# Splitting the first matmul of each seven-product group into two of 128 columns

## The chip, the cores and the metric

The kernel runs on one core of one Trainium2 chip. The metric is the device time of one execution in microseconds (us); the time of a kernel is the median of its runs.

## What is computed

The reference is a decoder trunk of two layers on 512 tokens of width 1024, in float32. Each layer has three sublayers, and the change lies in the first and the third of them, the half feed-forward networks (FFN):

```python
def swiglu(x, w_in, w_out):
    gate, up = jnp.split(x @ w_in, 2, axis=-1)
    return (jax.nn.silu(gate) * up) @ w_out

for l in range(DEPTH):
    h = layer_norm(ALPHA * h + 0.5 * swiglu(h, ffn1_in[l], ffn1_out[l]), ln_g[l, 0], ln_b[l, 0])
    mix = hybrid_mixer(h, ...)
    h = layer_norm(ALPHA * h + mix, ln_g[l, 1], ln_b[l, 1])
    h = layer_norm(ALPHA * h + 0.5 * swiglu(h, ffn2_in[l], ffn2_out[l]), ln_g[l, 2], ln_b[l, 2])
```

The hidden width of an FFN is 2816, which is 22 tiles of 128 columns for the gate and 22 for the up branch.

## The kernel before, in words

**Three matmuls for one product.** Weights and activations are float32. Each is held as a high part in float32r, rounded by a copy on ScalarE (ACT), and a low part, the difference, made on VectorE (DVE) (`Weights.parts`, L130 to L132). `mm3` (L341 to L345) does one block product as three float32r matmuls: activations' high part by the weights' high part (L343), low by high (L344) and high by low (L345), or with the sides changed where activations are the stationary operand. Every matmul instruction is issued with a load of its stationary operand, 128 columns; the profile lists these loads as an engine of their own, PEld. The first two matmuls of an `mm3` have the same stationary operand, and each loads it.

**Seven products in place of eight.** Most of the first matmul of an FFN, `x @ w_in`, is done in groups of four weight tiles (two gate, two up) by a Strassen-like scheme. In each group the 2 by 2 block product of weights and activations is made from seven block products of sums of blocks. `ffn` (L510) calls `quad` (L675) once for each group: 7 times in the first FFN of a layer and 9 times in the second, so 32 times in all over the two layers. The sums of activation blocks are made once per FFN (`x_sums`, L629), the sums of weight blocks for each group on GpSimd (POOL) and DVE (`quad_item`, L163).

**One product.** The inner function `product(i, bank, item, half, start)` (L682) does one of the seven: for the two halves g (gate and up) and four blocks k of 128 rows it calls `mm3` on 256 columns of the accumulation bank, 24 matmuls of 256 columns. So a group has 168 matmuls. The order of the products in a group is fixed in the code (L699 to L710): 1 into bank `qa`, 5 into `qc`, 6 into `qb`, 2 into `qa`, 4 into `qd`, 7 into `qb`, 3 into `qc`. A start flag stands on the first matmul of a bank only (L691: `first` needs `start`, k = 0 and g = 0); it clears the marks of the whole bank, so that the first matmul on the other 256 columns, which has no flag, overwrites too.

**Order around the change.** The instructions of each engine run in the order in which the program issues them. After product 1 the closing work of the group before is issued (`before()`, ACT and DVE), then product 5 and so on. The split weights stand in a ring of slots in SBUF; a product's last use of an item frees its slot (`W.done`, L206) and so lets the next item be made. Items of the groups are placed 16 elements further in a slot than the plain units (`SHIFT`, L33, L105). In front of the groups of an FFN stand pairs of plain units with 512-column matmuls into `g` and `u` (`pair`, L528), and in front of these, at the change of sublayer, plain units with 256-column matmuls into `hd` (L469 to L476), with transposes into `tx` (L414) between them.

Other matmuls that the text speaks of: L1196 in the attention (float32r, 64 columns each, into `cs`), L1101 in the state-space part (plain float32, 128 columns each, into `sx`; there are 16 such instructions with `er` over the two layers, and the profile has 32 records of them, two for each), L1234 (float32r, 256 columns, right behind L1196).

Of the kernel before, what the change touches and what calls it, by code (L numbers as in the profile page):

```python
# [216 lines left out]
class Trunk:  # L217
# [457 lines left out]
    def quad(self, u, xs, ap, op, acts, before):  # L675


        nc, ve, W = self.nc, self.nc.vector, self.W
        at = {n: u + i for i, n in enumerate(Weights.QUAD)}
        ba, bb, bc, bd = (self.bank(n) for n in ("qa", "qb", "qc", "qd"))  # L680

        def product(i, bank, item, half, start):  # L682
            xh, xl = xs[i]
            for g in range(2):
                n = item if item == "x4" else item + "gu"[g]
                wh, wl = W.get(at[n])
                o = bank[:, 256 * g:256 * g + 256]
                for k in range(4):
                    w = slice(512 * (g if item == "x4" else half) + 128 * k,
                              512 * (g if item == "x4" else half) + 128 * k + 128)  # L690
                    first, last = start and k == 0 and g == 0, k == 3 and g == 1  # L691
                    self.mm3(o, wh[:, w], wl[:, w], xh[:, k], xl[:, k], first, last, not start)
                if (i, item) in ((6, "x2"), (2, "x1"), (3, "x3")) or (item == "x4" and g == 1):
                    W.done(at[n], full=True)

        vw = op.tile([128, 2, SEQ], F32, tag="vw", name="vw")
        u2 = op.tile([128, SEQ], F32, tag="u2", name="u2")
        v, w = vw[:, 0], vw[:, 1]
        product(1, ba, "x1", 0, True)  # L699
        if before:  # L700
            before()
        product(5, bc, "x2", 0, True)
        nc.scalar.activation(v, ba, AF.Copy)
        product(6, bb, "x2", 1, True)
        nc.scalar.activation(w, bc, AF.Copy)
        product(2, ba, "x1", 1, False)
        ve.tensor_tensor(u2, v, bb, op=ALU.add)  # L707
        product(4, bd, "x4", 0, True)
        product(7, bb, "x3", 0, False)
        product(3, bc, "x3", 1, False)  # L710

        def after():
            a = ap.tile([128, 2, SEQ], F32, tag="u", name="aq")
            acts.append(a)
            ve.tensor_tensor(v, v, bb, op=ALU.add)
            ve.tensor_tensor(w, w, v, op=ALU.add)
            ve.tensor_tensor(v, v, bd, op=ALU.subtract)  # L717
            ve.tensor_tensor(u2, u2, bc, op=ALU.add)
            g, p = slice(0, 256), slice(256, 512)
            nc.scalar.activation(a[:, 0, g], ba[:, g], AF.Silu)  # L720
            nc.scalar.activation(a[:, 1].rearrange("p (i n) -> p i n", i=2), vw[:, :, g], AF.Silu)
            nc.scalar.activation(a[:, 0, p], u2[:, g], AF.Silu)
            ve.tensor_tensor(a[:, 0, g], a[:, 0, g], ba[:, p], op=ALU.mult)
            ve.tensor_tensor(a[:, 1].rearrange("p (i n) -> p i n", i=2),
                             a[:, 1].rearrange("p (i n) -> p i n", i=2), vw[:, :, p], op=ALU.mult)
            ve.tensor_tensor(a[:, 0, p], a[:, 0, p], u2[:, p], op=ALU.mult)

        return after
# [947 lines left out]
```

## Time and profile before

| | us |
|---|---|
| median of 3 runs | 1900.32 |
| lowest and highest run | 1898.56 and 1900.52 |
| the profiled execution's own time | 1899.04 |
| span of its profile, first to last instruction | 1897.1 |

The profile is of one execution. Its span leaves out about 2 us at the two ends of the execution. Engines are named PE (TensorE's matmuls), PEld (TensorE's weight loads), DVE, ACT, POOL and SP. A timeline row gives the start and the duration of an instruction in us, its engine, line and operation, what it writes and reads, the shape, and in brackets the idle time of the engine ahead of it and what ended that. Matmuls overlap: the duration of one is longer than the distance to the next. The type is shown as f32 for float32 and float32r alike in matmul rows.

### The profile page before, as it was taken

The numbers are of one execution on the slowest core, as the hardware profiler recorded it, in microseconds if no ns is written. First come the engines' busy times: TensorE is split into PE (matmuls) and PEld (weight loads), VectorE is DVE, ScalarE is ACT, GpSimd is POOL, SyncE is SP. The second block draws the span as 40 slices with busy tenths as digits, with TensorE's granted clock in tenths as the row PEclk, the third lists the DMA queues.
The fourth block names the chain that finished last, engine by engine and source line by source line (L and its number), as shares of the span: only waits on it lengthen the run. The fifth ranks groups of instructions, "written<-read, shape, count | busy, mean of one in ns | idle before, by whom it ended". The sixth has DMA issues, their size and how long they took to land.

```text
span 1897.1 us, 30481 instructions
## 1 busy us (share of the span) xinstructions
PE 1875.3 (99%) x12164; PEld 1672.4 (88%) x12164; DVE 1372.8 (72%) x1926; ACT 810.6 (43%) x1388; POOL 527.4 (28%) x539
## 2 busy tenths in 40 slices
PE   9999999999999999999999999999999999999998
PEld 7999878888788999998899998788977889999886
DVE  8998524767976899864598984346779678999534
ACT  5444323135771444543234543231458614455430
POOL 3332940114321322300042329301223232232001
PEclk9999999999999999999999999999999999999999
DMA  7233434022112123343203333340311211332421
GB/s 254 90 111 113 129 111 144 32 94 68 56 37 98 62 96 111 112 169 125 85 23 112 112 125 93 128 138 21 115 46 45 84 51 67 112 112 90 167 89 45
DMA packets 57214, 183.59 MB, mean 97 GB/s; under 512 B 11248, under 2 KB 12016, under 8 KB 57072
## 3 DMA queue, kind: packets, MB, share of 16 engines
q1 hardware_dynamic: 57072, 181.64, 28.6%
q8 instruction: 96, 1.57, 0.3%
q14 instruction: 46, 0.38, 0.1%
HBM read 179.19 MB, written 2.10 MB: 96 GB/s over the span
## 4 chain that ended last, share of the span: by engine, by line
PE 81%; POOL 8%; DVE 7%; DMA 2%; issue 1%; ACT 1%; SPq 0%; DVEq 0%; ACTq 0%; POOLq 0%
PE o L491 26%; PE qb L345 3%; PE qb L343 3%; PE qb L344 3%; PE qa L345 3%; PE qa L343 3%; PE qa L344 3%; PE qc L345 3%; PE qc L343 3%; PE qc L344 3%; PE o L1314 2%; PE pt L1298 2%; PE qd L345 2%; PE qd L343 2%; PE qd L344 2%; DVE ring L132 1%
## 5 line engine op out<-in xcount | busy, mean ns | idle before, releaser
L132 DVE TENSOR_TENSOR ring<-st,ring 128x1024 fp32r<-128x1024 f32 (+1 forms) x257 | 358.3, 1402 | 255.3 <-ACT ring L131 252.9
L131 ACT ACTIVATE ring<-st 128x1024 fp32r<-128x1024 f32 (+1 forms) x257 | 269.9, 1054 | 364.4 <-PE o L491 148.2
L491 PE MATMUL o<-ring,ap 128*128 128x512 f32 x1440 | 331.4, 391 | 3.5 <-ACT ap L602 3.3
L491 PEld LDWEIGHTS o<-ring,ap 128*128 128x128 f32 x1440 | 271.0, 188 | 61.5 <-ACT ap L602 4.1
L383 POOL TENSOR_TENSOR mv<-mv,expo 128x1 f32<-128x1 f32 x24 | 35.6, 1481 | 577.3 <-DVE mv L382 577.3
L182 POOL TENSOR_TENSOR st<-st,sb 128x512 f32<-128x512 f32 x64 | 96.6, 1510 | 187.0 <-DVE ring L132 119.3
L343 PE MATMUL qb<-th,ring 128*128 128x256 f32 x512 | 144.4, 282 | 0.3 <-DVE u L707 0.3
L344 PE MATMUL qb<-tl,ring 128*128 128x256 f32 x512 | 144.3, 282 | 0.0
L345 PE MATMUL qb<-th,ring 128*128 128x256 f32 x512 | 144.2, 282 | 0.0
L343 PE MATMUL qa<-xh,ring 128*128 128x256 f32 x512 | 143.5, 280 | 0.0
L345 PE MATMUL qa<-xh,ring 128*128 128x256 f32 x512 | 143.5, 280 | 0.0
L344 PE MATMUL qa<-xl,ring 128*128 128x256 f32 x512 | 143.5, 280 | 0.0
L491 PE MATMUL o<-wh,ap 128*128 128x512 f32 x448 | 125.5, 391 | 0.0
L177 POOL TENSOR_TENSOR sumg<-sb 128x512 f32<-128x512 f32 x32 | 51.0, 1595 | 178.0 <-DMA sb<-in_ffn_in 178.0
L491 PEld LDWEIGHTS o<-wh,ap 128*128 128x128 f32 x448 | 83.5, 188 | 17.6 <-DVE vw L717 0.6
L344 PEld LDWEIGHTS qb<-tl,ring 128*128 128x128 f32 x512 | 98.8, 193 | 0.0
L344 PEld LDWEIGHTS qa<-xl,ring 128*128 128x128 f32 x512 | 98.0, 191 | 0.1
L343 PEld LDWEIGHTS qb<-th,ring 128*128 128x128 f32 x512 | 96.8, 189 | 0.5 <-issue 0.5
L345 PEld LDWEIGHTS qb<-th,ring 128*128 128x128 f32 x512 | 96.9, 189 | 0.0
L132 DVE TENSOR_TENSOR wl<-st,wh 128x1024 fp32r<-128x1024 f32 x51 | 62.8, 1239 | 47.1 <-ACT wh L131 46.9
L343 PEld LDWEIGHTS qa<-xh,ring 128*128 128x128 f32 x512 | 96.1, 188 | 0.2
L345 PEld LDWEIGHTS qa<-xh,ring 128*128 128x128 f32 x512 | 96.1, 188 | 0.0
(459 smaller groups left out, 5163.4 us busy)
## 6 DMA issues: line engine op xcount, KB each, us to landing
st<-in_ffn_in SPq DMA_DIRECT2D x110, 512.0 KB, 3.3
st<-in_ffn_out SPq DMA_DIRECT2D x88, 512.0 KB, 3.3
sb<-in_ffn_in SPq DMA_DIRECT2D x64, 512.0 KB, 3.2
st<-in_w_out SPq DMA_DIRECT2D x16, 512.0 KB, 3.8
st<-in_w_b SPq DMA_DIRECT2D x8, 512.0 KB, 4.4
st<-in_w_a SPq DMA_DIRECT2D x8, 512.0 KB, 5.0
ln_g<-in_ln_g SPq DMA_DIRECT2D x6, 512.0 KB, 4.0
ln_b<-in_ln_b SPq DMA_DIRECT2D x6, 512.0 KB, 5.9
```

The lines of the kernel that those rows point to most:

```text
L131: self.nc.scalar.activation(hi, t, AF.Copy)
L132: self.nc.vector.tensor_tensor(lo, t, hi.bitcast(F32), op=ALU.subtract)
L177: po.tensor_tensor(s[:, f], b[:, f], b[:, r], op=ALU.add)
L182: po.tensor_tensor(a[:, f], a[:, f], b[:, f], op=ALU.subtract)
L343: mm(out, lhsT=ah, rhs=bh, start=start, stop=False, skip_group_check=skip)
L344: mm(out, lhsT=ah, rhs=bl, start=False, stop=False, skip_group_check=skip)
L345: mm(out, lhsT=al, rhs=bh, start=False, stop=stop, skip_group_check=skip)
L383: nc.gpsimd.tensor_tensor(mv[:, 2:3], mv[:, 2:3], self.expo, op=ALU.pow)
L491: mm(ps[t][f], lhsT=a[:, q], rhs=w[:, 512 * f:512 * f + 512], start=(k == first and a is ah and w is wh), stop=end)
L1298: nc.tensor.transpose(ps[:, 128 * k:128 * k + 128], p[:, i, 128 * k:128 * k + 128], ident)
L1314: mm(o[64 * i:64 * i + 64], lhsT=self.v[:, b, k, 64 * g:64 * g + 64], rhs=pt[:, i, 128 * k:128 * k + 128], start=False, stop=b == 1 and k ...
```

## The change

In product 1 of each group (i = 1, which writes `qa` and always has `start`), the first `mm3` (g = 0, k = 0) is written out. Its first matmul, 256 columns, becomes two of 128 columns with the same stationary operand, the first with the start flag and the second without; the other two matmuls of that `mm3` are as before.

```diff
                     first, last = start and k == 0 and g == 0, k == 3 and g == 1
-                    self.mm3(o, wh[:, w], wl[:, w], xh[:, k], xl[:, k], first, last, not start)
+                    if i == 1 and g == 0 and k == 0:
+                        for c in (slice(0, 128), slice(128, 256)):
+                            nc.tensor.matmul(o[:, c], lhsT=wh[:, w], rhs=xh[:, k, c], start=c.start == 0, stop=False)
+                        nc.tensor.matmul(o, lhsT=wh[:, w], rhs=xl[:, k], start=False, stop=False)
+                        nc.tensor.matmul(o, lhsT=wl[:, w], rhs=xh[:, k], start=False, stop=False)
+                    else:
+                        self.mm3(o, wh[:, w], wl[:, w], xh[:, k], xl[:, k], first, last, not start)
```

## Rows read from the trace of the kernel before

**Rows 1.** The page's first part: busy us, share of the span, instructions.

```profile
PE 1875.3 (99%) x12164; PEld 1672.4 (88%) x12164; DVE 1372.8 (72%) x1926; ACT 810.6 (43%) x1388; POOL 527.4 (28%) x539
```

**Rows 2.** Timeline at the start of two neighbouring groups in the first FFN.

```profile
94.61 0.28 PE L343 MATMUL qa<-xh,ring 128*128 128x256 f32 x1
94.61 0.19 PEld L344 LDWEIGHTS qa<-xl,ring 128*128 128x128 f32 x1
94.72 0.28 PE L344 MATMUL qa<-xl,ring 128*128 128x256 f32 x1
...
113.65 0.28 PE L343 MATMUL qa<-xh,ring 128*128 128x256 f32 x1
```

**Rows 3.** Timeline: starts of the first group and of two in the second FFN.

```profile
51.32 0.28 PE L343 MATMUL qa<-xh,ring 128*128 128x256 f32 x1
...
689.27 0.28 PE L343 MATMUL qa<-xh,ring 128*128 128x256 f32 x1
...
709.06 0.28 PE L343 MATMUL qa<-xh,ring 128*128 128x256 f32 x1
```

**Rows 4.** Windows: length, busy PE, PEld, DVE, ACT, POOL (instructions touched); clock, DMA share, GB/s.

```profile
94.60:113.60 19.00, 19.00 (x170) 19.00 (x169) 17.13 (x21) 9.79 (x13) 6.99 (x4) 1.00 0.33 112
171.50:191.30 19.80, 19.80 (x170) 19.80 (x169) 15.09 (x22) 7.40 (x11) 0.00 (x0) 1.00 0.43 131
649.70:827.80 178.10, 178.10 (x1514) 178.10 (x1513) 156.16 (x176) 89.95 (x118) 47.35 (x32) 1.00 0.35 117
996.00:1134.50 138.50, 138.50 (x1177) 138.50 (x1176) 122.45 (x134) 68.62 (x89) 36.41 (x24) 1.00 0.34 113
1590.40:1768.50 178.10, 178.10 (x1513) 178.07 (x1512) 156.28 (x176) 88.70 (x117) 44.09 (x32) 1.00 0.33 110
1075.10:1094.90 19.80, 19.80 (x170) 19.80 (x170) 18.99 (x21) 10.05 (x13) 5.87 (x4) 1.00 0.34 107
78.50:82.90 4.40, 4.40 (x27) 4.40 (x26) 3.93 (x6) 2.90 (x5) 1.29 (x1) 0.61 0.18 57
```

**Rows 5.** PE's timeline around two waits inside the first two groups.

```profile
65.93 0.36 PE L343 MATMUL qb<-th,ring 128*128 128x256 f32 x1 [0.32 <-DVE u L707]
...
67.04 0.28 PE L343 MATMUL qb<-th,ring 128*128 128x256 f32 x1
67.16 0.28 PE L344 MATMUL qb<-tl,ring 128*128 128x256 f32 x1
...
78.14 0.39 PE L345 MATMUL qc<-th,ring 128*128 128x256 f32 x1 [2.20 <-DVE ring L132]
```

**Rows 6.** PE's timeline in the sixth group of the first FFN.

```profile
155.92 0.28 PE L344 MATMUL qc<-tl,ring 128*128 128x256 f32 x1
156.11 0.39 PE L345 MATMUL qc<-th,ring 128*128 128x256 f32 x1
```

**Rows 7.** Timeline of the 64-column matmuls (eight merged) and what follows them.

```profile
461.14 1.08 PE L1196 MATMUL cs<-kc,qs 128*128 128x64 f32 x8
...
462.02 0.30 PEld L1234 LDWEIGHTS s<-kk,qs 128*128 128x128 f32 x2
462.05 0.37 PE L1234 MATMUL s<-kk,qs 128*128 128x256 f32 x1
```

**Rows 8.** PE's timeline of plain float32 matmuls with 128 columns, two records each.

```profile
401.13 0.39 PE L1101 MATMUL sx<-s5u,er 128*128 128x128 f32 x2
401.36 0.39 PE L1101 MATMUL sx<-s5u,ei 128*128 128x128 f32 x2
```

**Rows 9.** PE's timeline of the 256-column matmuls into `hd` behind transposes.

```profile
609.70 0.36 PE L343 MATMUL hd<-xh,ring 128*128 128x256 f32 x1
...
611.21 0.28 PE L343 MATMUL hd<-xh,ring 128*128 128x256 f32 x1
611.33 0.28 PE L344 MATMUL hd<-xl,ring 128*128 128x256 f32 x1
```

## The prediction

> **What bounds the kernel now.** I read the page's first part first: TensorE (PE) is busy 1875.3 of 1897.1 us, VectorE (DVE) 72% [rows 1]. So a nanosecond added to the matmul stream moves the end, unless it falls ahead of a wait for something else, and one saved counts as long as the weights keep coming. The change touches only the stream of the 32 seven-product groups, 168 matmuls each (7 products of 2 halves, 4 blocks, 3 terms), so I looked next at its pace.
>
> The timeline gives it from start to start (the duration in a row, 0.28 us, contains pipeline depth and is not the pace). One group starts at 94.61 and the next at 113.65: 19.04 us, or 113.3 ns a matmul [rows 2]. Another starts at 689.27 and the next at 709.06: 19.79 us, or 117.8 ns [rows 3]. The work is the same, PE has no gap in either, and the granted clock is 1.00, the 2.4 GHz level, in both [rows 4]. So **the same stream runs at one of two paces**, 0.75 us a group apart. The windows over all groups of three FFNs are slow throughout: 178.1 us for 9 groups, 138.5 for 7 and 178.1 for 9 [rows 4]. With the last group of the first FFN, 19.8 us from 171.5, 26 of 32 are wholly slow.
>
> What sets the pace? Once taken up, it holds over group after group. The groups of each FFN follow a gap-free stream of 512-column matmuls (at 51.32 in the first, [rows 3]) and start slow. The pace changes only where the rhythm breaks. At 65.93 a matmul waits for DVE, with 0.32 us of idle time; a microsecond later the step from 67.04 to 67.16 belongs to a fast stream [rows 5]. At 78.14 another has waited 2.20 us for a weight, then the clock falls towards the 1.2 GHz level (0.61 on average from 78.5 to 82.9, [rows 4]); after both the pace is fast, as at 94.61. At 156.11 a matmul comes 0.19 us after the one before it, and from there on the stream is slow, as in the window from 171.5 [rows 4, 6]. So of four breaks inside groups (the clock's return is one) three ended fast.
>
> **The change, part by part.** The first instruction of each group (256 columns) becomes two of 128, each with its own load of the same weights: 32 more matmuls, 32 more loads, no DMA, nothing on other engines. The old waits move to the first half. The fourth instruction's wait for the low part of the weights comes some 0.1 us later, which helps. No wait is added, so nothing queues behind one.
>
> *Price of a half.* No 128-column matmul of this operand type (float32r) is in the trace. The nearest are the eight 64-column ones of L1196, 461.14 to 462.05: 0.114 us each, the start included; the steady step is 0.112 [rows 7]. That is as long as a fast step of 256 columns, so something other than columns limits it. What, the interval from a load's start to its own matmul's start tells: 0.03 us for L1234 (462.02 to 462.05), which has 64 columns in front, 0.11 us in the fast stream (94.61 to 94.72) with 256 in front [rows 2, 7]. It grows with the columns in front, so it is the streaming time of the matmul ahead. 64 columns stream in 0.03 us, and the step of 0.112 is the weight load's. A half must then cost 0.112 as well, by its load.
>
> Bounds: below, half of a fast step, 0.057 us, if its load hid completely; above, the plain float32 matmul of 128 columns, two records from 401.13 to 401.36, 0.23 us [rows 8]. I take 0.112, since L1196 has the same operand type.
>
> The Trainium skill (TensorE: Matmul & The Clock Gate, LDWEIGHTS) puts a load of 128 columns at 128/1.2 = 107 ns; L1196's step agrees. The same page (Back-to-back issue gap) gives 262 cycles for 256 columns and 134 for 128: by it alone the split costs 6 cycles a group, 2.5 ns, nothing in the sum. L1196's step speaks against that here.
>
> *Direct cost.* In a slow stream 2 x 0.112 - 0.118 = 0.106 us a group, in a fast one 0.111. The first two groups lie ahead of the wait that ends at 78.14, which is for DVE and hides them. That leaves 30 x 0.106 = **+3.2 us**. With the bounds' ends: 30 x (0.114 - 0.118) = -0.1, and 30 x (0.46 - 0.118) = +10.3 us.
>
> *What the break does to the pace.* This is the large term, and the trace shows no break of just this form. The halves are limited by loads, so the instruction after them starts out of step with its load, as after the waits. The effect lies between 0 and 0.75 us a group, and below zero by a third pace (second rival). I take the fast pace, because three of four breaks inside the groups ended there, and this one comes at every group. Some instructions pass until it has settled, say 0.02 us. A slow group then gains 0.75 - 0.11 - 0.02 = 0.62 us.
>
> *Sum.* 26 slow groups x 0.62 = 16.1. The group in which 156.11 lies has about 129 matmuls left there at 4.4 ns, 0.57, less 0.13: 0.4. The three fast groups ahead of it, from 94.61 on, lose 3 x 0.13 = 0.4. That is -16.1 us. DVE, which makes the low parts of the weights, is busy 156.16/9 = 17.4 us a group in the second FFN, but 19.0 in the group from 1075.1 [rows 4]. A period of 19.15 us holds the first and leaves nothing for the second, so I expect small waits for weights in the third FFN and take off 1 us. **-15 us**: from the profiled execution's 1899.0 to 1884. The median shown is 1.3 us above that execution, so on its scale 1885; without waits for weights and settling, 1881 on the lower side.
>
> **The rivals.** *The pace stays*, because the halves are too small a break. For it: neither a change of product nor of operand ever changes the pace. Against it: the 0.19 us step at 156.11, shorter than two halves, did. Then only the direct cost counts, +3.2, 1903.5. If the break also turns the three fast groups and part of a fourth slow, 3.2 x 0.75 = 2.4 more: 1906.
>
> *The break leads to a still slower pace: slower than before.* The matmuls of hd start after 128-column transposes, come off a break at 609.70, and settle at 0.120 us (611.21 to 611.33, [rows 9]). Of the trace's breaks this is the one most like ours. Against it: no group shows 0.120, and hd's weights are unshifted units of the ring, the groups' are shifted by 16 elements. Here it would be 30 x 168 x 2.2 ns = 11.1, plus 3.2, plus 2.4 for lost fast groups: +17, 1917. It decides from a mean pace of 117.1 ns on (0.106 us spread over 168 below 117.8): above it the change is slower, below it faster.
>
> *Only some groups change pace*, as other slots and operands meet the break: with half of them, 13 x 0.62 gained, 13 x 0.106 and 0.4 lost, about -6: 1894.
>
> *A half costs the plain float32 price*, pace unchanged: +10.3, 1911. The 0.03 us for 64 columns speaks against it.
>
> That the change does something else than it says gets nothing: the second half lands in columns that the first half's start flag has cleared, as the second 256 columns of each bank do now.
>
> **How the numbers follow.** Fast pace nearly everywhere 0.50; some groups 0.12; pace stays 0.20; slower pace 0.14; plain price 0.04. A measurement of this kernel tells about 0.2%, 3.8 us, from no change. The first two cases are faster: 0.62. Of "pace stays", 0.14 lies just within the bound and 0.06, with the fast groups lost, beyond it; with the last two, slower has 0.24. Low is 1881; the high end reaches over most of "pace stays", 1905. Left out are the 0.18 of the last two cases. The likeliest case alone has 1881 to 1888.
>
> **What would show it.** qa's first line should show 64 records of 128 columns, the halves 0.11 us apart, and groups should start 19.15 us apart in all FFNs. I am wrong if they start 19.9 apart (pace stays) or 20.3 (slower pace), if waits for DVE ahead of qc eat what the pace gives, or, on the price, if two halves take 0.45 us.

## The result and the profile after

The changed kernel takes **1885.99 us** (median of four runs, 1883.3 to 1888.0); the kernel before beside it takes 1899.44 (four runs, 1897.97 to 1900.52). The ratio is 0.9929, 95% interval 0.9916 to 0.9942. Eleven more runs of the old kernel and six of the changed one in a later series gave 1898.42 and 1882.26, ratio 0.9922 (0.991 to 0.9934). The profile below is of the run of 1888.0 us, the slowest of the changed kernel, with a span of 1886.2; against the span before of 1897.1 it is 10.95 shorter from the first to the last matmul.

The page's first part of the kernel after:

```profile
PE 1863.3 (99%) x12196; PEld 1660.2 (88%) x12196; DVE 1372.3 (73%) x1926; ACT 809.4 (43%) x1388; POOL 528.5 (28%) x539
```

There are 32 more matmuls and 32 more loads than in [rows 1], and PE is busy 12.0 us less. DVE, ACT and POOL did the same work. PE bounds the kernel as before; it got through more instructions in less time.

The timeline of PE at the start of a group in the second FFN of the kernel after, with the start of the next group, answers to [rows 2, 3]. L694 is the split matmul, its two halves merged into one row:

```profile
670.75 0.33 PE L694 MATMUL qa<-xh,ring 128*128 128x128 f32 x2
670.92 0.33 PE L695 MATMUL qa<-xl,ring 128*128 128x256 f32 x1
671.09 0.28 PE L696 MATMUL qa<-xh,ring 128*128 128x256 f32 x1
671.21 0.28 PE L343 MATMUL qa<-xh,ring 128*128 128x256 f32 x1
671.33 0.28 PE L344 MATMUL qa<-xl,ring 128*128 128x256 f32 x1
671.44 0.28 PE L345 MATMUL qa<-xh,ring 128*128 128x256 f32 x1
...
689.92 0.33 PE L694 MATMUL qa<-xh,ring 128*128 128x128 f32 x2
```

From start to start it is 19.17 us where [rows 3] had 19.79. Behind the split the steps are 0.17, 0.12, 0.12, 0.11; from there to the next group all are 113.3 ns on average (162 steps in 18.36 us from 671.56 to 689.92). In this trace 30 of the 32 groups run so from end to end, apart from short waits. The first two turn slow (117.8) at a wait, that of 0.87 us at 66.41 and that of 1.9 us for a weight with the half clock behind it; each time the split of the next group, at 72.14 and at 95.63, ends it.

Windows over the groups of the second, third and fourth FFN of the kernel after answer to [rows 4] (the columns are the same); the last three are of stretches in which the clock fell:

```profile
651.60:824.10 172.50, 172.50 (x1521) 172.42 (x1520) 155.11 (x175) 87.81 (x117) 46.92 (x32) 1.00 0.35 117
993.10:1127.60 134.50, 134.50 (x1184) 134.28 (x1183) 121.60 (x134) 68.74 (x89) 37.76 (x24) 1.00 0.34 114
1585.00:1757.40 172.40, 172.40 (x1522) 172.40 (x1521) 156.75 (x175) 87.37 (x116) 46.58 (x32) 1.00 0.34 113
269.40:276.20 6.80, 5.60 (x13) 4.45 (x14) 4.75 (x6) 5.09 (x7) 0.00 (x0) 0.54 0.66 228
78.30:81.70 3.40, 3.02 (x14) 3.02 (x15) 3.40 (x5) 2.00 (x4) 1.28 (x1) 0.56 0.23 89
1163.70:1167.10 3.40, 3.40 (x20) 3.40 (x20) 0.42 (x1) 1.79 (x3) 3.32 (x6) 0.57 0.66 183
```

The nine groups that took 178.1 us take 172.5; the seven that took 138.5 take 134.5. The clock is 1.00 in both. Aligning the two traces matmul by matmul, the change gains 5.4 us in the second FFN, 3.9 in the third and 5.6 in the fourth: 14.9. The profiled run kept 10.95 of it, because about 4 us went elsewhere: 0.2 in and ahead of the first FFN, 0.6 at a wait (0.46 of idle time) in the `o` matmuls at the end of the second FFN, and 3.1 at places whose code the change does not touch, 269.4 and 1163.7. There the kernel before has, in its own profile:

```profile
270.60:274.00 3.40, 3.36 (x9) 2.39 (x8) 2.80 (x4) 3.08 (x5) 0.00 (x0) 0.50 0.55 182
274.00:277.40 3.40, 3.40 (x16) 2.79 (x16) 2.88 (x4) 1.54 (x3) 0.00 (x0) 0.99 0.82 283
1165.00:1168.40 3.40, 3.40 (x23) 3.01 (x21) 1.82 (x3) 1.06 (x1) 3.40 (x5) 1.00 0.82 282
```

At half the clock (the 1.2 GHz level) a step of 256 columns took 0.213 us in place of 0.113 to 0.118 (in the group at 72.14), so each such stretch of 3.4 us costs up to 1.7 us, where PE is busy in it. The run after has one more of them at 269.4 and one more at 1163.7. The one at 1163.7 is there in the later trace of the changed kernel too, at 1158.2, and not in the one trace of the kernel before; whether it belongs to the change is not shown. The waits of PE after, at the top of their view:

```profile
PE o L491 <- ACT ap L602: 3.8, 2, 2.9
PE qc L345 <- DVE ring L132: 1.9, 1, 1.9
```

The first, 2.9 us long at 270.60, stood at 2.17 before. Neither wait is where the split is.

### The profile page after: what moved, and what is told of

The parts are those of the page before. It is cut to its first block, busy times and chain, and to the rows that moved or that the text cites. A ratio compares the mean times of both kernels' runs of the same rounds, so it can differ in the third digit from the quotient of the medians.

```text
span 1886.2 us, 30545 instructions
## 1 busy us (share of the span) xinstructions
PE 1863.3 (99%) x12196; PEld 1660.2 (88%) x12196; DVE 1372.3 (73%) x1926; ACT 809.4 (43%) x1388; POOL 528.5 (28%) x539
## 4 chain that ended last, share of the span: by engine, by line
PE 79%; DVE 8%; POOL 8%; DMA 3%; issue 2%; ACT 1%; SPq 0%; DVEq 0%; ACTq 0%; POOLq 0%
PE o L491 26%; PE qb L344 3%; PE qb L343 3%; PE qb L345 3%; PE qc L345 3%; PE qc L344 3%; PE qc L343 3%; PE qa L344 3%; PE qa L343 3%; PE qa L345 3%; PE o L1320 2%; DVE ring L132 2%; PE pt L1304 2%; PE qd L343 1%; PE qd L344 1%
## 5 line engine op out<-in xcount | busy, mean ns | idle before, releaser
L343 PE MATMUL qb<-th,ring 128*128 128x256 f32 x512 | 141.8, 277 | 0.9 <-DVE u L713 0.9
L345 PE MATMUL qb<-th,ring 128*128 128x256 f32 x512 | 141.6, 277 | 0.0
L343 PE MATMUL qa<-xh,ring 128*128 128x256 f32 x480 | 132.7, 276 | 0.0
L344 PE MATMUL qa<-xl,ring 128*128 128x256 f32 x480 | 132.6, 276 | 0.0
L345 PE MATMUL qa<-xh,ring 128*128 128x256 f32 x480 | 132.6, 276 | 0.0
L343 PEld LDWEIGHTS qa<-xh,ring 128*128 128x128 f32 x480 | 90.1, 188 | 0.0
L344 PEld LDWEIGHTS qa<-xl,ring 128*128 128x128 f32 x480 | 90.1, 188 | 0.0
L345 PEld LDWEIGHTS qa<-xh,ring 128*128 128x128 f32 x480 | 90.1, 188 | 0.0
```

Source lines behind the costliest of these rows:

```text
L343: mm(out, lhsT=ah, rhs=bh, start=start, stop=False, skip_group_check=skip)
L344: mm(out, lhsT=ah, rhs=bl, start=False, stop=False, skip_group_check=skip)
L345: mm(out, lhsT=al, rhs=bh, start=False, stop=stop, skip_group_check=skip)
```

## The experiments

All splits below are of the changed kernel's form (two halves, the other two matmuls of the `mm3` as they were). Starts and steps are read from PE's timeline of each run. Where no number of runs stands with a time, it is that of one run. The cuts from the code show the lines that matter; `...` stands for the lines that only carry a flag or a number there.

### Does the pace hold by itself? One split in an FFN

```diff
-                late = self.quad(self.unit_at["quad", kind, l, j], xs, ap, op, acts, late)
+                late = self.quad(self.unit_at["quad", kind, l, j], xs, ap, op, acts, late, j == q0)
...
-                    if i == 1 and g == 0 and k == 0:
+                    if i == 1 and g == 0 and k == 0 and kick:
```

> The split only in the first group of each FFN (4 splits in place of 32). Theory: the pace is a state that holds until the rhythm breaks, so one split serves all groups behind it; these start 19.04 us apart with no 0.13 us for a split, and the time is some 28 x 0.13 = 3.6 us under the changed kernel's, about 1882 us; where a wait for weights breaks the rhythm a group may fall back to 19.79 us. Rival: a split acts on its own group alone; then only 4 groups are fast, the others start 19.79 us apart, and the time is about 1897 us.

1886.34 us, median of four (1885.35 to 1890.26), against 1898.33 before on that chip: ratio 0.9936 (0.992 to 0.9953). The timeline of PE, with two group starts of the second FFN and a wait in the fourth:

```profile
666.95 0.28 PE L343 MATMUL qa<-xh,ring 128*128 128x256 f32 x1
...
685.99 0.28 PE L343 MATMUL qa<-xh,ring 128*128 128x256 f32 x1
...
1605.83 0.38 PE L345 MATMUL qc<-th,ring 128*128 128x256 f32 x1 [0.23 <-DVE ring L132]
...
1621.24 0.28 PE L343 MATMUL qa<-xh,ring 128*128 128x256 f32 x1
...
1641.03 0.28 PE L343 MATMUL qa<-xh,ring 128*128 128x256 f32 x1
```

By the time, four splits are not told apart from 32 (ratio 0.9929 and 0.9922). The unsplit groups behind the first are 19.04 apart, exactly the fast group of [rows 2]: the pace, once taken up, stays. So it is a state of the stream, not a property of the split instructions. My 1882 was too low for two reasons. At 19.04 the stream overruns DVE now and then, as the prediction had feared for the third FFN: the group at 705.03 took 19.58, with a wait for DVE in it (0.26 us of idle time). And such a wait is a break too, which can end either way: those in the groups at 92.45, 1103.70 and 1601.13 ended slow (the last is shown: 19.79 from 1621.24 to 1641.03), and nothing set the pace right again until the next FFN. Eleven groups ran wholly slow by it. Splitting every group is a repair at each one; splitting one is cheaper but leaves the relapses.

### Is it the additional instruction? The first matmul twice, whole

```diff
-                        for c in (slice(0, 128), slice(128, 256)):
-                            nc.tensor.matmul(o[:, c], lhsT=wh[:, w], rhs=xh[:, k, c], start=c.start == 0, stop=False)
+                        for n in range(2):
+                            nc.tensor.matmul(o, lhsT=wh[:, w], rhs=xh[:, k], start=n == 0, stop=False)
```

> In each group the first matmul is done twice with all 256 columns (its block product is added twice, so the output is not the reference's): one more instruction and one more load as in the changed kernel, but none that is limited by its load. Theory (the short step limited by its load is what moves the pace): the groups stay slow, 19.90 us apart, about 1903 us. Rival (any additional instruction does it, for instance because a group then has an odd number): 19.17 us apart, about 1886 us.

1900.59 us. PE's timeline at two group starts:

```profile
667.46 0.40 PE L694 MATMUL qa<-xh,ring 128*128 128x256 f32 x2
...
687.37 0.28 PE L694 MATMUL qa<-xh,ring 128*128 128x256 f32 x1
```

19.90 a group: 169 steps of 117.8, the slow pace throughout the last three FFNs. In the first FFN, where waits had made the groups fast, they stayed fast (19.15). One more instruction of the same length changes neither pace: of the 26 that met a slow stream or opened an FFN, none ended fast. What counts is the short one.

### Does the place in the group matter? The form of the split?

```diff
...
-                    if i == 1 and g == 0 and k == 0:
+                    if (i == 6 or i == 1 and kick) and g == 0 and k == 0:
```

> The split moved from product 1 to product 6 (10 us later in the group, behind the place where the groups wait for weights), and in the first group of each FFN also in product 1: 36 splits. Theory: the pace is a state, so the place of the split in the group doesn't matter: groups 19.17 us apart as in the changed kernel, 1886 us; a group that a wait for weights (before the 38th matmul) turns slow is fast again from the 49th on and loses under 0.1 us where the changed kernel loses up to 0.6. Rival (the split works by the change of group, or by product 1's operands): groups at 19.9 us, over 1897 us.

1886.08 us; 19.17 a group with the split at product 6, in all of the last three FFNs, but for waits and for the first group of each, which has two splits (19.30). Those first groups are fast by the split in product 1, so most splits in product 6 have nothing to repair. Four do: the groups at 112.56, 150.98, 782.28 and 1028.02 turn slow at a small wait and fast at the split some ten matmuls behind it. PE's timeline of the third:

```profile
786.86 0.28 PE L344 MATMUL qc<-tl,ring 128*128 128x256 f32 x1
...
787.80 0.33 PE L694 MATMUL qb<-th,ring 128*128 128x128 f32 x2
...
788.37 0.28 PE L344 MATMUL qb<-tl,ring 128*128 128x256 f32 x1
...
797.89 0.28 PE L344 MATMUL qb<-tl,ring 128*128 128x256 f32 x1
```

Eight steps in 0.94 us ahead of the split are 117.5 ns each, 84 steps in 9.52 behind it 113.3. The place in the group does not matter.

```diff
-                        for c in (slice(0, 128), slice(128, 256)):
+                        for c in (slice(0, 64), slice(64, 256)):
```

> The changed kernel with the first matmul split into 64 and 192 columns in place of 128 and 128. Theory: both pieces are shorter than a weight load, each costs a load, and the stream behind them starts out of step with its loads as before: 19.17 us a group, 1886 us, two pieces 0.22 us. Rival (only equal halves hit the fast pace): groups at 19.9 us, about 1901 us.

1883.2 us (one run). PE's timeline:

```profile
1006.32 0.36 PE L694 MATMUL qa<-xh,ring 128*128 128x64 f32 x2
1006.52 0.31 PE L695 MATMUL qa<-xl,ring 128*128 128x256 f32 x1
1006.66 0.28 PE L696 MATMUL qa<-xh,ring 128*128 128x256 f32 x1
```

The 64 columns take 0.03 us until the second piece starts, which then takes 0.17, and L695 0.14: together 0.34, as with 128 and 128 (0.06, 0.11, 0.17). Groups are 19.17 apart again. So the cost of a split is not that of its columns: both cuts cost 0.13 over the 19.04 of an unsplit group, about one more load of 0.11. But the split does not always bring the fast pace: the group at 1025.48 turned slow at a wait of under 0.1 us, the next, at 1045.31, took up its split (steps of 0.029, 0.175, 0.136) and went on at 117.8, 19.89 in all; the one after it was fast.

### The third pace: hd split as well

```diff
-            self.m_tile(u0 + i, hp[i], 0, 256)
+            self.m_tiles([u0 + i], [hp[i]], 0, 256, i != 1)
...
+                if kick and k == 0:
+                    mm = self.nc.tensor.matmul
+                    for c in (c0, c0 + 128):
+                        mm(p[:, c:c + 128], lhsT=wh[:, w], rhs=self.xh[:, k, c:c + 128], start=c == c0, stop=False)
+                    mm(p[:, c0:c1], lhsT=wh[:, w], rhs=self.xl[:, k, c0:c1], start=False, stop=False)
+                    mm(p[:, c0:c1], lhsT=wl[:, w], rhs=self.xh[:, k, c0:c1], start=False, stop=False)
+                    continue
```

> The changed kernel, with the same split also in the 256-column matmuls into hd, in the first matmul of three of the eight tiles of each of the three places (at the start and behind each block of transposes): 9 more splits. Theory: hd's step goes from 0.120 to 0.113 us; 576 matmuls x 0.0067 = 3.8 us less 9 x 0.11 for the splits: about 2.9 us faster than the changed kernel. Rival (the third pace belongs to the place of the weights in the ring, not to the history): 0.120 us again a few steps behind each split, and 1 us slower.

1886.39 us. PE's timeline, ten matmuls behind the split at 611.30:

```profile
612.56 0.28 PE L343 MATMUL hd<-xh,wh 128*128 128x256 f32 x1
612.68 0.28 PE L344 MATMUL hd<-xl,wh 128*128 128x256 f32 x1
```

0.120, as in [rows 9]. My theory fell: `hd` settles at 0.120 whatever it comes off, and no split moves it. The rival, that the weights' place makes the third pace, was left.

### The place alone: groups without the offset, with and without the split

The kernel before, and then the changed kernel, with the groups' items placed like the plain units:

```diff
-        o = 0 if kind == "unit" else SHIFT
+        o = 0
```

> The kernel before, without a split, with the groups' items not shifted by 16 elements in their slots. If the place of the weights decides on the third pace: groups 168 x 0.120 = 20.16 us apart, 32 x 0.37 = 12 us slower than before, about 1911 us. If only the history decides, the groups start as before, 19.79 us apart, about 1899 us.

1924.67 us. PE's timeline without the split:

```profile
719.61 0.28 PE L343 MATMUL qa<-xh,ring 128*128 128x256 f32 x1
719.73 0.28 PE L344 MATMUL qa<-xl,ring 128*128 128x256 f32 x1
...
739.77 0.28 PE L343 MATMUL qa<-xh,ring 128*128 128x256 f32 x1
```

> The changed kernel (32 splits) with the groups' items not shifted in their slots. Theory after the unshifted kernel without a split ran all groups at 0.120 us: the place of the weights sets which paces there are, and the split only chooses between the two that the shifted place has. Then the groups stay at 0.120 us a matmul, at least 20.25 us apart, and the time is 1915 us or more. Rival (a split leads to the fast pace wherever the weights stand): 0.113 us, 19.17 us apart but for waits, under 1900 us.

1921.85 us. PE's timeline with it:

```profile
696.39 0.34 PE L694 MATMUL qa<-xh,ring 128*128 128x128 f32 x2
696.56 0.33 PE L695 MATMUL qa<-xl,ring 128*128 128x256 f32 x1
...
716.65 0.22 PE L694 MATMUL qa<-xh,ring 128*128 128x128 f32 x1
```

The step is 0.120 in every group, with the split and without, after waits of about 3 us too: where nothing is waited for, a group takes 168 x 0.120 = 20.16 without the split and 20.26 with it. At this place there is one pace and nothing to win by a break. Against slow groups the place costs 32 x 0.37 = 12 us; most of the rest of the 26 us are waits inside the groups, 14 us by their starts (8.0 of idle time at `qb` for DVE's `u` alone).

The kernel before with another offset:

```diff
-SHIFT = 16
+SHIFT = 8
```

> The kernel before with the items of the groups placed 8 elements further instead of 16; no split. If any offset against the plain units is enough, the groups step at the same two paces as before: 19.79 us apart in the later FFNs, 1899 in all. Rival: an offset of 8 elements counts as none, as in the run without an offset: steps of 0.120 us, 20.16 us apart or more, about 1924. A third outcome, 19.04 apart from the start of each FFN, would mean that the slow pace belongs to the offset of 16 and not to the rhythm: about 1882. I hold the first two equally likely and the third at one in ten.

1903.79 us. PE's timeline at two group starts:

```profile
710.79 0.28 PE L343 MATMUL qa<-xh,ring 128*128 128x256 f32 x1
...
730.67 0.28 PE L343 MATMUL qa<-xh,ring 128*128 128x256 f32 x1
```

None of the three outcomes: 19.88 a group, 118.3 ns a step, in all 32 groups, also behind the wait of 1.76 us at 78.06 after which the groups of the kernel before step at 113.3. At 0 elements one pace is seen (120.0), at 8 one (118.3), at 16 two (117.8 and 113.3). A split was tried at 0 and at 16, not at 8, so a faster pace at 8 is not excluded. The ring is 8 elements shorter here as well, which moves what lies behind it; `hd`, `g` and `u` kept their steps.

### Can hd have it as well? Three tries

First the four units of `hd` alone are moved by 16 elements, on top of the split in `hd`:

```diff
-        o = 0 if kind == "unit" else SHIFT
+        o = 0 if kind == "unit" and i not in self.shifted else SHIFT
...
```

> The kernel with 9 splits in hd, with hd's four units also shifted by 16 elements in their slots as the groups' items are. If the place sets the third pace: hd's step falls from 0.120 to 0.113 us (0.118 where no split reaches it), up to 3.8 us less than with the splits alone, 1883 us. Rival: hd keeps 0.120 us, because of its activations or its transposes, and the time stays at 1886 us; weights that stand outside the ring can keep it in part.

1886.98 us. PE's timeline:

```profile
612.56 0.28 PE L344 MATMUL hd<-xh,ring 128*128 128x256 f32 x1
612.67 0.28 PE L345 MATMUL hd<-xl,ring 128*128 128x256 f32 x1
...
631.68 0.50 PE L344 MATMUL u<-xh,ring 128*128 128x512 f32 x1 [0.57 <-ACT ring L131]
...
635.44 0.80 PE L346 MATMUL u<-xh,ring 128*128 128x512 f32 x1 [3.03 <-DVE ring L132]
```

`hd` now steps at 113.3, and its three sections of a place take 22.31 us in place of 23.50 in the run with the split alone, so 3 x 1.19 = 3.6 are won (2.6 against the changed kernel, which has no splits in `hd` and takes 23.17). They are lost again in front of the second FFN's groups: there `u` comes 6 us later than in the run with the split alone. Of that 3.6 are waits for weights, most of the rest is a stretch at half the clock behind them:

```profile
633.60:640.40 6.80, 4.96 (x12) 3.94 (x13) 6.80 (x8) 3.75 (x5) 0.00 (x0) 0.53 0.52 183
```

The planner's order of the weights changed with the place: a moved unit may not use the extra slot (`wh` and `wl`, which `hd` had at 612.56 above), and reaches 16 elements into the slot behind its own.

So next every unit in the ring was moved, with the splits in `hd` kept and the extra slot allowed for plain units as before:

```diff
-        o = 0 if kind == "unit" else SHIFT
-        for s in sorted(range(self.slots - (o > 0)), key=lambda s: self.freed[s]):
+        o = SHIFT
+        for s in sorted(range(self.slots - (kind != "unit")), key=lambda s: self.freed[s]):
```

> The kernel with hd's splits, and now every weight in the ring is placed 16 elements further, plain units too, which keep the slot that the other run with hd's units moved had forbidden them. Theory: hd's sections take 22.3 us in place of 23.5 at each of three places (unless a unit lies in the extra slot), no 3 us wait for weights comes in front of u, because that came from the slot; 1886.4 less up to 3.6: 1883, and against the kernel with the change alone 0.998 to 1.000. Rival: the faster hd itself makes the weights late: the wait in front of u (3.0 us, with half clock behind it) comes again, 1887.

1892.67 us, median of five (1889.78 to 1892.82), ratio to before 0.9966 (0.9954 to 0.9978), and 10.4 over the changed kernel on the same chip. The wait in front of `u` is gone, as the theory had it, and `hd` gained 0.5 us a place (1.2 if it stepped at 113.3 throughout: one unit of each place lay in the extra slot and stepped at 0.120, and the units behind it went on at 117.8). But the plain units lost more. One of the lines of `u` in the view by line, first from the run with `hd` split and nothing moved:

```profile
L344 PE MATMUL u<-xl,ring 128*128 128x512 f32 x144 | 56.0, 389 | 0.0
```

and from this one:

```profile
L344 PE MATMUL u<-xl,ring 128*128 128x512 f32 x144 | 57.0, 396 | 0.0
```

7 ns more for each matmul of 512 columns. From start to start, worked out over each trace, `u` steps at 233 ns in place of 227 (405 steps), `g` at 232.7 for 228.2 (403) and `o` at 229.7 for 228.1 (2472): 2.7 + 1.8 + 4.0 = 8.5 us. What 16 elements give the 256-column stream they take from the 512-column ones. Two groups also stayed slow through their split (19.89 at 645.58 and 1582.95), 1.4 us.

Last, plain units at their old place and `hd`'s at the new one in every slot, with the two tiles of the extra slot 16 elements wider for it:

```diff
...
-            return tuple(self.split.tile([128, 1024], F32R, tag=g, name=f"{g}{i}") for g in self.extra)
+            o = SHIFT if i in self.shifted else 0
+            return tuple(self.split.tile([128, 1024 + SHIFT], F32R, tag=g, name=f"{g}{i}")[:, o:o + 1024] for g in self.extra)
```

> Plain units at their old place, hd's four units at the place of the groups (16 elements further) in every slot, the extra slot too, whose two tiles are 16 elements wider for that. Theory: hd steps at 113.3 ns in all its sections (22.3 us a place against 23.5), the 512-column streams at 227 ns again (the run with all units moved had up to 235), no 3 us wait for weights in front of u in the third FFN, since that came from the slot that was forbidden to hd: 3.6 us under the changed kernel, a ratio to before of 0.990 to 0.991. Rival: the weights in front of u come late again because hd is faster, 0.993 as the changed kernel. What I can't exclude: the wider first tile moves the second one by 16 elements, and units with their low parts there may step otherwise.

1915.67 us, median of six (1913.77 to 1921.58), ratio 1.0093 (1.0076 to 1.0111): slower than the kernel before. The view by line:

```profile
L500 PE MATMUL o<-ring,ap 128*128 128x512 f32 x1440 | 338.5, 395 | 0.8 <-ACT ap L611 0.5
```

Here `o` steps at 233.2 ns, 5 over the changed kernel's 228.0 on 2476 steps, 13 us, and `g` and `u` lose 5 ns a step as well (some 400 steps each); 13 of the 32 groups are slow in spite of their splits, two of them from a wait on; and there are waits for weights of 4.5 us at `g` in front of the second FFN and 3.0 at `u` in front of the fourth. So the forbidden slot, which `hd` may use here, was not all that made the weights late. This run shares with the first of the three that `hd`'s units reach 16 elements into the slot behind; that alone was not tried. A tile 64 bytes wider in each partition moved what lies behind it, and the streams that were at their best before no longer are. Which tile's place did it was not tried.

### The changed kernel again

> The changed kernel as it is, for a comparison beside the run before it on one chip: a median of 1886, from 1883 to 1888, as in its first runs, and a ratio to before of 0.993. Where a run lies between those ends goes by the number of windows at about half clock in it: two of them 1884 or lower, four 1888.

1882.26 us, median of six (1880.08 to 1886.8). What I expected of the half clock fell short. The profiled run, the fastest, has three such stretches of about 3.4 us besides its end; the run of 1888.0 has them at three places with one twice as long, about 13.7 us in all, so 1.7 us of the 7.9 between the two. The larger part lies at one place, where the windows of this run show

```profile
269.40:276.20 6.80, 6.80 (x32) 5.63 (x31) 5.81 (x7) 4.55 (x6) 0.00 (x0) 1.00 0.75 254
```

no idle time and the clock at 1.00, where the first run had the wait of 2.9 us for ACT and 6.8 us at half the clock: 6.1 us between them, worked out from the starts around it (0.2 us apart at 230, 6.3 at 332). So one wait that comes or does not, with the clock behind it, makes most of the difference between these two runs. Four of the groups' late steps ended slow over the two traces, six fast; the smallest that ended slow was a single step of 0.13 us, in this run's group at 112.35.

## Why the prediction was right

**The level.** 1885 was forecast and 1886 measured, with faster by 0.7%. The gain of 15 us stood against 13.5 in the first series and 16.2 in the second.

**The price of a half** was right in the sum, not in its parts. The steps were not 0.112 and 0.112: the second half follows 0.06 after the first (it was to be 0.11), L695 0.11 later, L696 0.17 after that. The three steps make 0.34, as forecast (0.112 + 0.112 + 0.113). The timeline of the loads (PEld) of the kernel after, around the start at 670.75, says why:

```profile
670.53 0.19 PEld L345 LDWEIGHTS qc<-xh,ring 128*128 128x128 f32 x1
670.64 0.30 PEld L694 LDWEIGHTS qa<-xh,ring 128*128 128x128 f32 x2
670.86 0.19 PEld L695 LDWEIGHTS qa<-xl,ring 128*128 128x128 f32 x1
670.97 0.19 PEld L696 LDWEIGHTS qa<-xh,ring 128*128 128x128 f32 x1
```

They go on 0.11 apart straight through the split. The first half's short step is the 0.057 of the lower bound, but the loads behind it cannot follow, so the debt is paid two instructions later. The 64 and 192 columns of the other cut gave the same sum. In the fast stream the split thus costs 19.17 - 19.04 = 0.13 us, the 0.11 and 0.02 of the forecast. The cycles of the Trainium skill (TensorE: Matmul & The Clock Gate, Back-to-back issue gap), by which two halves would cost, as an estimate, 2.5 ns more than the whole, are given there for an isolated matmul, and the section itself says that they under-count small ones in a stream with loads. That is so here: the split cost 130 ns. The 107 ns of the Trainium skill (same page, LDWEIGHTS) for a load of 128 columns is near the 0.11 measured.

**The break and the pace**, the large term, came out at the forecast size: 19.79 to 19.17 is 0.62 a group, the number of the sum. The period of 19.15 was 0.02 short. The reason given, a rhythm between loads and matmuls that a short instruction upsets, is supported by three runs: one split per FFN suffices, a whole additional instruction does nothing, the place in the group is indifferent. That this break ends fast rested on three of four breaks in the trace before, which were waits and a change of the clock. Four breaks are few to go by, and waits turned out to be another matter: in the two traces of the changed kernel they ended fast in six of ten cases. So the odds taken were in part luck. The split did better: all 11 that met a slow stream or opened an FFN in these two traces ended fast. It is still not certain: a run each with 64 columns, with everything moved and with the wider tiles has groups that kept 117.8 through their split. One reading was incomplete, too: behind the 0.19 us step at 156.11, which the prediction called shorter than two halves, there is a second late one (the row after [rows 6] starts 0.22 later):

```profile
156.33 0.28 PE L343 MATMUL qc<-th,ring 128*128 128x256 f32 x1
```

What the rhythm is, the loads tell in part. Their view by line, in ns, first in a slow group before (700 to 718), then in a fast one after (672 to 689):

```profile
L344 PEld LDWEIGHTS qb<-tl,ring 128*128 128x128 f32 x16 | 3.1, 192 | 0.0
L343 PEld LDWEIGHTS qb<-th,ring 128*128 128x128 f32 x16 | 3.0, 188 | 0.0
```

```profile
L344 PEld LDWEIGHTS qb<-tl,ring 128*128 128x128 f32 x16 | 3.0, 188 | 0.0
```

In both a load starts 2 to 5 ns behind the matmul ahead of it, so a lasting shift between loads and matmuls is not what tells the paces apart. But in the slow groups every third load takes 192 ns, in the fast ones none, and without the offset, at 120.0, all do. In the run with the first matmul doubled, where a group has 169 instructions, the long load moves on by one term from group to group: the count of three goes on through the stream. The slow groups of the run with wider tiles have no such load, so it is a mark of the slow pace, not shown to be its cause. And the two paces were seen at one place of the weights only. Why at 16 elements there are two stays open.

**Waits for weights** were put at 1 us, in the third FFN. The groups at 766.58, 1031.39 and 1108.22 took 0.17, 0.17 and 0.24 longer than 19.17, and the wait at the end of the second FFN cost 0.6: together 1.2, with the places only half right. That 19.15 would nearly do and 19.04 would not fits the run with one split per FFN, where waits in the groups at 705.03 and 1027.12 cost 0.54 and 0.41 and the others made the stream slow.

**The first FFN** was to gain 0.6 by its last, wholly slow group, with the rest of it even. Its groups gained 0.16 and, with 0.33 lost ahead of them, it came out at +0.2. The first two groups were taken to be hidden by the wait that ends at 78.14; they lost 0.35 each, because the waits at 66.41 and 78.68 ended slow this time.

**The rivals.** "Pace stays" is what the whole additional instruction shows: 1900.59, slower for an instruction that breaks nothing. "A slower pace" exists, 120.0 ns, but not behind a break: it is that of unmoved weights. I had named this as the argument against the rival and given it 0.14; the argument was right, as the runs without the offset show. The plain float32 price was out of the question, with 0.11 a load.

**What was not in the sum:** the clock. The forecast took the run's half-clock stretches as given. They differ between runs, at 270 with a wait of 0 to 2.9 us in front of them, and that wait and its clock make 6.1 us between the two traces of the changed kernel, more than one FFN's groups gained. The medians came out 1 us above the forecast in one series and 3 below it in the other, so the nearness of the first is in part luck.

## What to carry to other kernels

When PE is busy without a gap and its clock is full, read the pace of the stream from start to start, and compare stretches of the same shape with each other: a stream of 256-column float32r matmuls had 113.3, 117.8, 118.3 or 120.0 ns here. If one shape shows two paces, a short instruction in the stream is a cheap test; and where the weights lie is a size to try like any other, for each stream by itself, because what suits one can cost another more. A gain in pace is only kept where the suppliers keep up, and where waits can undo it, a repair in every group has to be weighed against its 0.13 us: here one split per FFN and one per group came out alike.

## What was not expected of the hardware

- The pace of a stream depends on where its weights lie. With 256 columns the steps were 120.0 ns at 0 elements, 118.3 at 8 (without a split), and 117.8 or 113.3 at 16. With 512 columns they were 227 at 0 and up to 233 at 16.
- At one place two paces are both stable over hundreds of matmuls, and the slow one is marked by a load of 192 ns in every three, the others being 188: nine groups, 1512 steps, at 117.8 in the kernel before; the same nine, but for the split and one short wait, at 113.3 in the run with one split.
- A matmul of 64 columns let the next one start 0.03 us later, and one of 128 columns 0.06, with the loads still 0.11 apart: a few short matmuls run ahead and wait afterwards.
- Widening two tiles by 64 bytes a partition and placing `hd` anew made the kernel 0.9% slower than the kernel before, by 5 ns on each of the 2476 steps of `o` and some 400 each of `g` and `u`, and by late weights.
